# Four engines in a written order around attention and the Fourier mixer of a two-layer diffusion kernel

## The chip, the cores and the metric

The kernel is one program on one core of a Trainium2 chip. The core has five engines that run side by side, each working through its own list of instructions: PE (TensorE, matrix products; its weight loads are shown apart as PEld), DVE (VectorE), ACT (ScalarE), POOL (GpSimd) and SP (SyncE), which here only issues transfers. The metric is the device time of one execution in microseconds, from the first to the last moment of the program on the chip.

## What is computed

Two layers over 256 tokens of width 1024, in float32. Each layer is a mixer and a mixture of experts, both scaled, shifted and gated by "ada" vectors that come from a conditioning vector:

```python
for layer in range(2):
    mod = silu(c) @ ada_w[layer] + ada_b[layer]          # 6 vectors of 1024
    shift1, scale1, gate1, shift2, scale2, gate2 = split(mod, 6)
    h = modulate(rmsnorm(x, norm_mix[layer]), shift1, scale1)
    if layer == 0:
        q, k, v, xb, gb = split(h @ w_in)                # plus context keys and values
        attn = neighbourhood_attention(q, k, v, k_c, v_c, rpb)
        y = bidirectional_rglru(xc_lat, xc_ctx, ...)     # a scan in each direction
        mix = concat([attn, gelu(gb) * y]) @ w_out
    else:
        f = fft2(h in 4 channel groups, ortho).real      # over tokens and channels
        mix = f @ fnet_w_out
    x = x + gate1 * mix
    h2 = modulate(rmsnorm(x, norm_ffn[layer]), shift2, scale2)
    x = x + gate2 * grouped_moe(h2, ...)                 # best of 4 groups, its top 2 of 4 experts
```

## The kernel before, in words

Weights stream from memory through 16 slots of 1 MB in one fixed list that SP works off in order; a transfer starts when the slot that it needs has been released by its reader. A chunk of ada weights takes two slots and gives four columns of an ada vector (`modc`). A chunk is turned into numbers in one of three ways: on PE by 64 small products `gv` into one row, a copy to ACT's `gvr` and a second product that turns the row (`side(1)` takes one such chunk per attention unit, from the list `ADA`); on PE in the router by `fill` (the lists `FILL0`, `FILL1`); or on DVE in the slot itself with a column sum on PE (the list `BESIDE`).

The stages stand one behind the other. First the projections and the scan. Then attention in 20 units u: scores `s` in pairs, on DVE a bias add and a maximum `mx`, on ACT the exponential `P`, on DVE its division, on PE the transposes `pt`, copied by ACT to `PT`, and every fourth unit the product `av` of four units, which ACT and DVE (or POOL) split into a high and a low part `catH`, `catL`. From unit 6 on, one step of the output projection `mix` per unit stands between them: six products of 512 columns with a weight piece `wp` whose high part ACT copies and whose low part POOL or DVE subtracts, by the letters g and v of a string (`EO` in attention, `EF` in the Fourier mixer). Then the residual add (`gm`, `xt`), the norm, the router's logits `lg`, scores `sc`, the choice of experts `oh`, ranks `rk`, a selection matrix `S`, and the first gather `xg`, whose rows go to the first products `g`. Then eight pairs of experts (`g`, `u`, `dn`, scatter `ya`). Layer 1 begins with the Fourier mixer: `dr` (the transform matrix times the norm), `f`, `Y`, then `pq`, `pc`, `pn`, from which ACT and DVE make `fH` and `fL`, then sixteen `mix` steps; then the same router and experts.

What sets the order: PE's instructions stand as the program writes them from the projections to the end of the output projection (`by_hand`, line 699). All else, and the other engines throughout, is placed by a scheduler in the order in which it estimates that things become ready. The small row `dg`, made by POOL from an ada vector, is what PE turns into the gate row `gb` that ACT copies to `gate` for the residual add.

Of the kernel before, what the change touches and what calls it, by code (L numbers as in the profile page):

```python
# [36 lines left out]
ORDER = 'aaKaaBaGaaVaaapoa'  # L37
# [6 lines left out]
EF = 'vvggggvggvvggvgg'  # L44
# [101 lines left out]
def hybrid_layers(  # L146
# [73 lines left out]
    def exp_items(l):  # L220
# [137 lines left out]
    def ada_pe(l, j, ps_=gps, after=None):  # L358
        W = st.get(("a", l, j))
        return ada_te(l, [(W, q * 128, 4 * j + q) for q in range(4)], ps_=ps_, after=after, used=W.used)  # L360

# [10 lines left out]
    def ada_inplace(l, j):  # L372
# [4 lines left out]
        for k in range(1, 8):  # L377
            ve.scalar_tensor_tensor(r, W[:, k], sc32[:, k, 0:1], r, op0=ALU.mult, op1=ALU.add)
        W.done(1)
        yield  # L380
        p = wps("gv")
        for q in range(4):
            te.matmul(out=p[:, q:q + 1], lhsT=r[:, q * 128:(q + 1) * 128], rhs=ones[:, 0:1], start=True, stop=True)
        c4 = slice(4 * j, 4 * j + 4)
        ve.tensor_tensor(modc[l][:, c4], p[:, 0:4], ada_b[l][:, c4], op=ALU.add)
        W.done(0)
        yield
# [176 lines left out]
    st.add([ada_item(*a) for n in FILL0 for a in n])  # L564
# [134 lines left out]
    by_hand.enter_context(tc.manual_schedule(engines={mybir.EngineType.PE}))  # L699
# [51 lines left out]
    scan[1](99)  # L751
# [90 lines left out]
    def project(srcH, srcL, W, order, on):  # L842

        p = [acc("mix") for _ in range(4)]
        steps = [(k, h) for k in order for h in range(2)]
# [9 lines left out]
        for i, (k, h) in enumerate(steps):  # L855
            if i + 2 < 16:
                w[i + 2] = piece(i + 2)
            if i < 14:
                for tb in range(2):
                    c = slice(tb * 128, (tb + 1) * 128)  # L860
                    mm3(p[tb * 2 + h], (srcH[:, k, c], srcL[:, k, c]), w[i], i < 2, False)
            elif i == 15:
                for tb in range(2):
                    c = slice(tb * 128, (tb + 1) * 128)
                    for h in range(2):
                        mm3(p[tb * 2 + h], (srcH[:, k, c], srcL[:, k, c]), w[14 + h], False, True)
# [4 lines left out]
    mix = project(catH, catL, lambda h: st.get(("wo", h)), (4, 5, 6, 7, 0, 1, 2, 3), EO)  # L871
# [10 lines left out]
    gate = gate_rows(0, 16)  # L882
    for mp in mix:
        pass
    by_hand.close()


    def warm(n):

        p = gps("warm")  # L890
        for _ in range(n):
            te.matmul(out=p[:, 0:352], lhsT=ones, rhs=cst, start=True, stop=True)

    def add_mix(p4, gate):

        table(AF.Sqrt, p4[0][:, 0:1])
        ss = tn([128, 2, 2], "ssq")
        for h in range(2):
            c = slice(h * 512, (h + 1) * 512)
            for tb in range(2):  # L900
                add_gated(p4[tb * 2 + h], gate, tb, c)
                jk = t2k("jk")[:, 0:256].bitcast(BF16)
                ac.activation(jk, xt[:, tb, c], AF.Square, accum_out=ss[:, tb, h:h + 1])
        r = tn([128, 2], "rr", bufs=2)
        ve.tensor_tensor(r, ss[:, :, 0], ss[:, :, 1], op=ALU.add)
        ac.activation(r, r, AF.Sqrt, scale=1.0 / D, bias=eps)
        last = ve.reciprocal(r, r)
        return r, last

    def moe(l, r, store):  # L910
        a2 = scale_col(f"a2_{l}", modc[l], 32, g_ffn[l])
        b2 = modc[l][:, 24:32]

# [4 lines left out]
                         b2[:, :, None].to_broadcast([128, 8, 16]), op=ALU.mult)  # L918
# [4 lines left out]
        pre = table(AF.Sigmoid, r[:, 0:1])  # L923
        fins = fill(l, 0, pre)
        if not fins:
            warm(5)

        xT = t8k("xT").rearrange("p (k t) -> p k t", k=8)
        lg = acc("lg")
        lv = lg[:, 0:32].rearrange("p (t e) -> p t e", t=2)  # L930
        for kk in range(4):
            p = wps("tp")
            for i in range(4):
                k = 2 * kk + i // 2
                te.transpose(p[:, i * 128:(i + 1) * 128], xt[:, i % 2, k * 128:(k + 1) * 128], ident)
            pv = p.rearrange("p (k t) -> p k t", k=2)
            if kk % 2:
                ve.tensor_copy(xT[:, 2 * kk:2 * kk + 2], pv)
            else:
                ac.activation(xT[:, 2 * kk:2 * kk + 2], pv, AF.Copy)  # L940
        for k in range(8):
            for tb in range(2):
                at = te.matmul(out=lv[:, tb], lhsT=xT[:, k, tb * 128:(tb + 1) * 128], rhs=w2[:, k],
                               start=(k == 0 and tb == 0), stop=(k == 7 and tb == 1))
        for f in fins:
            f()
        with tc.issue_after(at.ins):
            fins = fill(l, 1, pre)
# [3 lines left out]
        for tb in range(2):  # L952
            ac.activation(xh[:, tb], xt[:, tb], AF.Copy, scale=r[:, tb:tb + 1])
            ve.scalar_tensor_tensor(xl[:, tb], xt[:, tb], r[:, tb:tb + 1], xh[:, tb].bitcast(F32),
                                    op0=ALU.mult, op1=ALU.subtract)
        sc = tn([128, 2, NE], "sc")
        for tb in range(2):
            ve.scalar_tensor_tensor(sc[:, tb], lv[:, tb], r[:, tb:tb + 1], crow, op0=ALU.mult, op1=ALU.add)
        ac.activation(sc, sc, AF.Sigmoid)
        table(AF.Silu, sc[:, 0, 0:1])  # L960
# [31 lines left out]
        warm(3)  # L992
# [6 lines left out]
        rank = tn([128, 2, NE], "rank")  # L999
        ve.scalar_tensor_tensor(rank, rk[:, 0:32].rearrange("p (t e) -> p t e", t=2), 1.0, oh, op0=ALU.add, op1=ALU.mult)  # L1000
# [5 lines left out]
        at = ve.scalar_tensor_tensor(over, rank, float(CAP), gates, op0=ALU.is_gt, op1=ALU.mult)  # L1006

        with tc.issue_after(at.ins):
            for f in fins:
                f()  # L1010
        sg_of = {}

        def gather(b):


            e = 4 * b
            S = t2k("S")[:, 0:512].bitcast(F32R)
# [360 lines left out]
```

## Time and profile before

| what | us |
|---|---|
| three runs, median (lowest, highest) | 807.3 (803.17, 809.81) |
| the profiled execution, its own time | 808.83 |
| its span, first to last instruction | 807.0 |
| attention and output projection, from the first scores | 172.9 to 247.35 |
| router of layer 0 and first gather | 247.35 to 274.27 |
| experts of layer 0 | 274.27 to 511.2 |
| Fourier mixer | 511.2 to 558.93 |
| router of layer 1 and first gather | 558.93 to 585.5 |
| experts of layer 1 and the store | 585.5 to 807.0 |

Times in the table after the third row are positions in the span, read from the trace. The profiled execution lies 1.5 us over the median, so a sum made against it is lowered by 1.5 us to compare it with the median.

### The profile page before, as it was taken

To read this page: it belongs to the slowest core of one execution; us is meant where nothing else is said; L and a number is where in the kernel's file an instruction comes from. 1 tells how busy PE (TensorE), PEld (TensorE's weight loads), DVE (VectorE), ACT (ScalarE), POOL (GpSimd) and SP (SyncE) were. 2 spreads that over 40 slices of the span, in tenths; PEclk is the share of its full clock that TensorE was granted. 3 is DMA by queue.
4 is the path that set the end of the run, shared out by engine and by line. 5 is a ranking of instruction groups with operands and counts; after the bars stand their busy time and mean duration, and the time that the engine had idled before them with its cause. 6 is when DMAs were issued, how large, how long until landed. Compare 5 with 4: busy or idle time off the path is not lost. (4 is left out here: it accounts for less than half of the span.)

```text
span 807.0 us, 11360 instructions
## 1 busy us (share of the span) xinstructions
PE 726.8 (90%) x4602; PEld 398.8 (49%) x4602; DVE 291.8 (36%) x577; ACT 243.8 (30%) x435; POOL 124.4 (15%) x107
## 2 busy tenths in 40 slices
PE   3999987976999899799999879699899799999996
PEld 2677576554777534244334324467643343444334
DVE  4558279185634321021143231444421110221115
ACT  6253975944556111010011000354310100110001
POOL 1146254353240001000000000023000000000002
PEclk8899999997999999899999989899899999999999
DMA  8999843495468799999999999974579999999995
GB/s 280 361 356 403 337 167 130 183 358 212 163 257 344 292 424 421 378 422 421 422 421 421 421 421 421 420 305 156 210 305 422 418 386 423 421 421 421 422 402 181
DMA packets 53793, 277.40 MB, mean 344 GB/s; under 512 B 4898, under 2 KB 20832, under 8 KB 22496
## 3 DMA queue, kind: packets, MB, share of 16 engines
q1 hardware_dynamic: 53008, 275.95, 85.4%
q8 instruction: 40, 0.66, 0.3%
q10 hardware_dynamic: 720, 0.59, 0.2%
q14 instruction: 25, 0.20, 0.1%
HBM read 275.47 MB, written 1.05 MB: 343 GB/s over the span
## 5 line engine op out<-in xcount | busy, mean ns | idle before, releaser
L1085 PE MATMUL g<-slot,xg 128*64 128x512 f32 x512 | 122.2, 627 | 13.3 <-PEq L1193 8.2
L1085 PE MATMUL u<-slot,xg 128*64 128x512 f32 x512 | 115.2, 593 | 3.9 <-DMA slot<-in_moe_u_dram 3.9
L1122 PE MATMUL dn<-slot,aT 128*64 128x512 f32 (+1 forms) x544 | 115.4, 571 | 3.2 <-DVE aT L1106 3.2
L392 POOL TENSOR_TENSOR wp<-slot,wp 128x512 fp32r<-128x512 f32 x52 | 73.5, 1420 | 157.0 <-ACT wp L391 156.9
L1085 PEld LDWEIGHTS g<-slot,xg 128*64 128x64 f32 x512 | 39.3, 145 | 91.9 <-issue 83.8
L1091 DVE TENSOR_TENSOR act<-act,u 128x512 f32<-128x512 f32 x16 | 11.0, 687 | 199.2 <-PE u L1085 199.2
L1085 PEld LDWEIGHTS u<-slot,xg 128*64 128x64 f32 x512 | 37.6, 137 | 78.1 <-issue 69.8
L1122 PEld LDWEIGHTS dn<-slot,aT 128*64 128x64 f32 x544 | 37.6, 137 | 69.0 <-issue 60.8
L1124 ACT ACTIVATE yH<-dn,gcol 128x512 fp32r<-128x512 f32 (+1 forms) x34 | 22.5, 662 | 139.1 <-PE dn L1122 133.7
L1042 POOL TENSOR_TENSOR SG<-S,gates 128x512 f32<-128x512 f32 x8 | 8.4, 1045 | 355.0 <-PE st L1094 307.3
L1040 ACT ACTIVATE xg<-xg,modc,a 128x256 f32<-128x256 f32 x32 | 18.0, 564 | 135.8 <-PE xg L1031 135.8
L1125 DVE SCALAR_TENSOR_TENSOR yL<-dn,gcol,yH 128x512 fp32r<-128x512 f32 (+1 forms) x34 | 24.4, 719 | 89.7 <-ACT yH L1124 81.5
L334 PE MATMUL gv<-slot,sc 128*32 128x128 f32 x1344 | 51.3, 292 | 4.0 <-ACT sc L307 2.0
L391 ACT ACTIVATE wp<-slot 128x512 fp32r<-128x512 f32 x72 | 44.5, 626 | 30.3 <-PE mix L406 9.3
L1090 ACT ACTIVATE act<-g 128x512 f32<-128x512 f32 x16 | 9.6, 597 | 132.9 <-PE g L1085 132.9
L334 PEld LDWEIGHTS gv<-slot,sc 128*32 128x32 f32 x1344 | 42.1, 118 | 14.5 <-issue 7.0
L1031 PE MATMUL xg<-S,xh 128*128 128x256 f32 x128 | 27.3, 295 | 3.3 <-DVE S L1019 2.1
L1038 DVE TENSOR_SCALAR xg<-xg,a,modc 128x256 f32<-128x256 f32 x32 | 17.4, 543 | 31.8 <-ACT xg L1040 31.8
L1062 PE MATMUL ya<-yH,ST 128*128 128x512 f32 x60 | 26.4, 440 | 0.3 <-ACT yH L1124 0.2
L1031 PE MATMUL xg<-S,xl 128*128 128x256 f32 x128 | 25.9, 284 | 0.0
L1062 PE MATMUL ya<-yL,ST 128*128 128x512 f32 x60 | 24.1, 402 | 0.6 <-DVE yL L1125 0.6
L392 DVE TENSOR_TENSOR wp<-slot,wp 128x512 fp32r<-128x512 f32 x20 | 16.9, 846 | 20.7 <-ACT wp L391 20.5
(269 smaller groups left out, 1101.0 us busy)
## 6 DMA issues: line engine op xcount, KB each, us to landing
slot<-in_moe_g_dram SPq DMA_DIRECT2D x64, 1024.0 KB, 14.2
slot<-in_moe_u_dram SPq DMA_DIRECT2D x64, 1024.0 KB, 15.1
slot<-in_moe_d_dram SPq DMA_DIRECT2D x60, 1024.0 KB, 16.2
slot<-in_ada_w_dram SPq DMA_DIRECT2D x40, 1024.0 KB, 8.3
slot<-in_w_in_dram SPq DMA_DIRECT2D x8, 1024.0 KB, 12.4
slot<-in_ada_w_dram SPq DMA_DIRECT2D x12, 512.0 KB, 9.1
slot<-in_w_out_dram SPq DMA_DIRECT2D x4, 1024.0 KB, 7.2
slot<-in_fnet_w_dram SPq DMA_DIRECT2D x4, 1024.0 KB, 19.8
```

The costliest lines, as they stand in the source:

```text
L334: te.matmul(out=p[32 * q:32 * q + 32, 0:128], lhsT=sc32[:, k, :], rhs=W[:, k, c:c + 128], start=(k == 0), stop=(k == 7))
L391: ac.activation(dst_h, src, AF.Copy)
L392: eng.tensor_tensor(dst_l, src, dst_h.bitcast(F32), op=ALU.subtract)
L1031: at_xg[0] = te.matmul(out=p[:, i * 256:(i + 1) * 256], lhsT=xx[:, tb, k * 128:(k + 1) * 128], rhs=S[:, tb * 256:(tb + 1) * 256], start=(n ...
L1038: ve.tensor_scalar(xg[:, k], pv, a2[:, k:k + 1], b2[:, k:k + 1], op0=ALU.mult, op1=ALU.add)
L1040: ac.activation(xg[:, k], pv, AF.Identity, scale=a2[:, k:k + 1], bias=b2[:, k:k + 1])
L1062: te.matmul(out=yacc[tb * 2 + h], lhsT=ST[:, tb * 128:(tb + 1) * 128], rhs=y[:, h * 512:(h + 1) * 512], start=(p == 0 and n == 0), stop=(n ...
L1085: te.matmul(out=q[half(i), :], lhsT=xg[:, k, half(i0 + i)], rhs=W[i][:, k], start=(k == 0), stop=(k == 7))
L1091: ve.tensor_tensor(act, act, gu[1], op=ALU.mult)
L1122: te.matmul(out=dn[half(i), :], lhsT=aT[:, fc * 128 + 64 * i:fc * 128 + 64 * i + 64], rhs=W[i][:, fc, c], start=(fc == 0), stop=(fc == 3))
L1124: ac.activation(yH[:, c], dn, AF.Copy, scale=gcol)
L1125: ve.scalar_tensor_tensor(yL[:, c], dn, gcol, yH[:, c].bitcast(F32), op0=ALU.mult, op1=ALU.subtract)
```

## The change

All four computing engines now keep the order in which the program writes their instructions, in two stretches: from the first attention unit to the first gather of layer 0, and from the Fourier mixer's start to the first gather of layer 1. The last nine steps of the second scan direction are called from units 0 to 2, three each. The output projection starts one step later against the units (13 steps beside units and not 14); residual adds are taken apart by half of the width (`add_part`), and in the Fourier mixer the steps are ordered so that the first half is done four steps before the end. The router's weights are made ready ahead of the norm, its products are taken in halves, and its filling products (`warm`) are fewer. Of the ada chunks two move into the list that attention takes (13 and not 11), three and not four are taken in the router of layer 0, and the last two are loaded behind the Fourier weights and reduced by DVE beside the mixer, where three were loaded among the experts of layer 0 and reduced there.

```diff
-ADA = [(0, 4), (0, 5), (0, 6), (0, 7), (0, 8), (0, 9), (1, 0), (1, 2), (1, 1), (1, 3), (1, 6)]
-FILL0 = [[(0, 10), (0, 11)], [(1, 4), (1, 5)], []]
-FILL1 = [[], [(1, 10), (1, 11)], []]
-BESIDE = [(1, j) for j in (7, 8, 9)]
-EF = 'vvggggvggvvggvgg'
+ADA = [(0, 4), (0, 5), (0, 6), (0, 7), (0, 8), (0, 9), (1, 0), (1, 2), (1, 1), (1, 3), (1, 6), (1, 7), (1, 4)]
+FILL0 = [(0, 10), (0, 11), (1, 5)]
+FILL1 = [(1, 10), (1, 11)]
+BESIDE = [(1, 8), (1, 9)]
+EF = 'gggvggvggvggvggv'
...
-            if l == 0 and n == "d" and p - 4 in range(len(BESIDE)):
-                r.append(ada_item(*BESIDE[p - 4]))
...
     st.add([st.chunk(("fw", h), fnet_w[h]) for h in range(2)])
-    st.add([ada_item(*a) for n in FILL1 for a in n])
+    st.add([ada_item(*a) for a in BESIDE + FILL1])
...
-    by_hand.enter_context(tc.manual_schedule(engines={mybir.EngineType.PE}))
+    by_hand.enter_context(tc.manual_schedule(engines={te.engine}))
+    engines = {te.engine, ve.engine, ac.engine, gp.engine}
...
-    scan[1](99)
+
+    by_hand.close()
+    by_hand.enter_context(tc.manual_schedule(engines=engines))
...
     for u in range(20):
         att()
-        if u < 6:
+        if u < 10:
             side(1)
-        if 2 <= u < 6:
+        scan[1](3 if u < 3 else 0)
+        if 3 <= u < 7:
             cat()
         if u >= 6:
-            mp = next(mix)
+            next(mix)
...
+        def low(h, tb):
+            c = slice(h * 512, (h + 1) * 512)
+            ve.scalar_tensor_tensor(xl[:, tb, c], xt[:, tb, c], r[:, tb:tb + 1], xh[:, tb, c].bitcast(F32),
+                                    op0=ALU.mult, op1=ALU.subtract)
...
-    warm(8)
-    r, _ = add_mix(yacc, gate)
+    by_hand.enter_context(tc.manual_schedule(engines=engines))
...
+    for tb in range(2):
+        add_part(yp, gate, 0, tb)
+    add_part(yp, gate, 1, 0)
+    warm(6, xt[:, 1, 0:352])
+    e0 = first_half()
+    rms(r, e0, 0)
+    add_part(yp, gate, 1, 1)
+    warm(4, xt[:, 0, 512:864])
+    rms(r, e0, 1)
...
+    group(0)
+    group(1)
+    next(mix)
     gate = gate_rows(1, 16)
-    for mp in project(fH, fL, lambda h: st.get(("fw", h)), range(8), EF):
-        pass
-    r, _ = add_mix(mp, gate)
-    moe(1, r, True)
+    lg = Logits()
+    for n, mp in enumerate(mix):
+        beside(1)
+        if n in (10, 11):
+            ada_sum(*BESIDE[n - 10])
+        if n == 11:
+            table(AF.Sqrt, eps)
+            for tb in range(2):
+                add_part(mp, gate, 0, tb)
+        if n == 12:
+            a2, crow = router_weights(1)
...
+    moe(1, mp, gate, lg, a2, crow, True)
```

ACT in the second half of attention, before (line 788 is the exponential of one unit, 804 the copy `PT`, 391 a high part):

```order
L788 ACTIVATE P,sm<-s,mx 128x512 x2
L391 ACTIVATE wp<-slot_1567 128x512
L804 ACTIVATE PT<-pt 128x4x128
L391 ACTIVATE wp<-slot_1567 128x512
L804 ACTIVATE PT<-pt 128x4x128
L788 ACTIVATE P,sm<-s,mx 128x512 x2
```

The same place of the kernel after (808, 824 and 408 are those lines there):

```order
L808 ACTIVATE P,sm<-s,mx 128x512
L824 ACTIVATE PT<-pt 128x4x128
L408 ACTIVATE catH<-av 128x256
L408 ACTIVATE wp<-slot_1628 128x512
L808 ACTIVATE P,sm<-s,mx 128x512
L824 ACTIVATE PT<-pt 128x4x128
L408 ACTIVATE wp<-slot_1628 128x512
```

Two exponentials stood side by side ahead of the pieces; now a copy `PT` and a piece `wp` stand between the two exponentials of every pair.

POOL at the start of the Fourier mixer's `mix`, before (420 is the gate's `dg`, 392 a low part; `SG` belongs to the experts ahead of it):

```order
L1042 TENSOR_TENSOR SG<-S,gates 128x512 x2
L420 TENSOR_TENSOR dg<-cst,modc_141 128x1024
L392 TENSOR_TENSOR wp<-slot_6878,wp 128x512 x2
L392 TENSOR_TENSOR wp<-slot_6880,wp 128x512 x3
```

POOL at the same place, after (437 and 409 are those lines):

```order
L1081 TENSOR_TENSOR SG<-S,gates 128x512 x2
L409 TENSOR_TENSOR wp<-slot_6874,wp 128x512 x2
L437 TENSOR_TENSOR dg<-cst,modc_141 128x1024
L409 TENSOR_TENSOR wp<-slot_6876,wp 128x512
```

ACT there, after:

```order
L1387 ACTIVATE fm<-pn 1x2x127
L408 ACTIVATE fH<-fm 128x2x256 x2
L408 ACTIVATE wp<-slot_6874 128x512 x2
L443 ACTIVATE gate<-gb 128x512 x2
L408 ACTIVATE wp<-slot_6876 128x512 x2
```

And PE there, after (1374 to 1376 are the last transform products, 421 to 423 the first `mix` step):

```order
L1374 MATMUL pq<-Y,dft 128x254
L1375 MATMUL pc<-Y,dft 128x258
L1376 MATMUL pn<-Y,dft 32x258
L442 MATMUL gb<-dg,cst 128x512 x2
L421 MATMUL mix<-wp,fH 128x512
L422 MATMUL mix<-wp,fH 128x512
L423 MATMUL mix<-wp,fL 128x512
```

The gate's `dg` stood on POOL ahead of the low parts, with nothing of the mixer before it; now it stands behind the first two low parts, whose high parts stand on ACT behind the last `fH`, and on PE the gate's products stand ahead of the first `mix` step.

## Rows read from the trace of the kernel before

**Rows 1.** Windows: us; busy PE, PEld, DVE, ACT, POOL; PEclk; DMA share; GB/s.

```profile
193.00:247.35 54.35, 52.63 (x408) 37.20 (x407) 26.69 (x64) 31.10 (x67) 16.05 (x12) 1.00 0.63 241
247.35:274.27 26.92, 24.31 (x354) 20.11 (x353) 15.10 (x45) 12.21 (x25) 1.05 (x1) 0.87 0.93 371
274.27:511.20 236.93, 220.18 (x1021) 90.76 (x1020) 56.99 (x97) 26.65 (x43) 6.92 (x5) 0.97 0.99 409
511.20:528.20 17.00, 9.52 (x34) 7.99 (x34) 9.47 (x25) 6.61 (x18) 1.27 (x1) 0.80 1.01 421
528.20:535.50 7.30, 7.30 (x29) 3.87 (x28) 3.15 (x9) 3.74 (x11) 0.00 (x0) 1.00 1.02 423
535.50:558.93 23.43, 23.01 (x98) 18.05 (x97) 8.46 (x13) 10.75 (x22) 11.71 (x9) 1.00 0.54 185
558.93:585.50 26.57, 22.94 (x233) 18.32 (x232) 13.78 (x41) 11.55 (x23) 1.05 (x1) 0.87 0.43 172
585.50:807.00 221.50, 207.36 (x1021) 86.43 (x1020) 46.49 (x87) 24.82 (x41) 10.00 (x8) 0.98 0.95 385
```

**Rows 2.** PE's timeline at attention's start: start, us, engine, line, operation.

```profile
173.96 1.95 PE L334 MATMUL gv<-slot,sc 128*32 128x128 f32 x64
187.01 0.47 PE L342 MATMUL gv<-cst,gvr 128*128 128x128 f32 x1 [11.10 <-ACT gvr L340]
187.41 2.39 PE L776 MATMUL s<-kq 64*128 64x256 f32 x8
189.74 3.15 PE L334 MATMUL gv<-slot,sc 128*32 128x128 f32 x64
```

**Rows 3.** PE's timeline in the steady units of attention.

```profile
207.64 1.14 PE L776 MATMUL s<-kq 64*128 64x256 f32 x8
208.70 0.66 PE L803 MATMUL pt<-cst,P 128*128 128x128 f32 x4
```

**Rows 4.** Groups by line on ACT, 193 to 247.35: busy, mean ns, idle before.

```profile
L391 ACT ACTIVATE wp<-slot 128x512 fp32r<-128x512 f32 x16 | 9.9, 627 | 3.8 <-PE mix L406 2.2 <-PE av L811 1.5
L804 ACT ACTIVATE PT<-pt 128x512 f32<-128x512 f32 x16 | 9.5, 596 | 14.0 <-PE pt L803 10.9 <-PE av L811 3.0
L788 ACT ACTIVATE P<-s,mx 128x512 f32<-128x512 f32 x12 | 8.1, 683 | 1.1 <-DVE mx L785 0.9
```

**Rows 5.** Groups by line on DVE, same stretch.

```profile
L785 DVE TENSOR_REDUCE mx<-s 128x1 f32<-128x512 f32 x12 | 7.7, 680 | 0.0
...
L783 DVE TENSOR_TENSOR s<-s,bg 128x256 f32<-128x256 f32 x12 | 4.8, 428 | 3.6 <-PE s L776 3.6
```

**Rows 6.** Groups by line on POOL, same stretch.

```profile
L392 POOL TENSOR_TENSOR wp<-slot,wp 128x512 fp32r<-128x512 f32 x11 | 14.2, 1295 | 38.5 <-ACT wp L391 38.5
L420 POOL TENSOR_TENSOR dg<-cst,modc 128x1024 f32<-128x1024 f32 x1 | 1.9, 1897 | 1.9 <-PE av L811 1.9
```

**Rows 7.** PE's timeline: the last product of layer 1's experts.

```profile
801.75 0.28 PE L1072 MATMUL z<-yL,ST 128*128 128x256 f32 x1
```

**Rows 8.** PE's timeline in the Fourier mixer.

```profile
518.70 9.49 PE L1260 MATMUL f<-dr,xt 128*128 128x257 f32 x32 [7.48 <-DVE dr L1251]
```

**Rows 9.** DVE's timeline in the Fourier mixer.

```profile
526.49 0.35 DVE L1262 TENSOR_SCALAR Y<-f,a 128x129 f32<-128x129 f32 x1 [0.32 <-PE f L1260]
527.35 0.35 DVE L1262 TENSOR_SCALAR Y<-f,a 128x129 f32<-128x129 f32 x1 [0.32 <-PE f L1260]
...
535.64 0.68 DVE L392 TENSOR_TENSOR fL<-fm,fH 128x512 fp32r<-128x512 f32 x1
537.32 1.36 DVE L392 TENSOR_TENSOR fL<-fm,fH 128x512 fp32r<-128x512 f32 x1 [1.00 <-ACT fH L391]
```

**Rows 10.** POOL's timeline in the Fourier mixer.

```profile
536.85 1.29 POOL L392 TENSOR_TENSOR wp<-slot,wp 128x512 fp32r<-128x512 f32 x1 [23.33 <-ACT wp L391]
```

**Rows 11.** PE's timeline in the router of layer 1.

```profile
564.53 4.79 PE L892 MATMUL warm<-cst 128*128 128x352 f32 x10
```

**Rows 12.** DVE's timeline in the router of layer 1.

```profile
571.19 2.47 DVE L954 SCALAR_TENSOR_TENSOR xl<-xt,rr,xh 128x1024 fp32r<-128x1024 f32 x2
```

More of the change, by code (lines that the diff above doesn't have):

```diff
@@ L386, in ada_inplace, with ada_parts @@
         W.done(0)
+    def ada_parts(l, j, p, stops=()):
+        W = st.get(("a", l, j))
+        for k in range(8):
+            for q in range(4):
+                te.matmul(out=p[32 * q:32 * q + 32, 0:128], lhsT=sc32[:, k, :], rhs=W[:, k, q * 128:(q + 1) * 128],
+                          start=(k == 0), stop=(k == 7))
+            W.used(k)
+            if k in stops:
+                yield
+        yield
+        r = t1k("gvr")
+        ac.activation(r[:, 0:128], p[:, 0:128], AF.Copy)
+        yield
+        te.transpose(p[:, 128:256], r[:, 0:128], ident)
+        yield
+        c4 = slice(4 * j, 4 * j + 4)
+        ve.tensor_tensor(modc[l][:, c4], p[:, 128:256:32], ada_b[l][:, c4], op=ALU.add)
         yield
@@ L840, in add_gated, with project @@
         eng.tensor_tensor(xt[:, tb, c], xt[:, tb, c], m[:, 0:n], op=ALU.add)
-    def project(srcH, srcL, W, order, on):
-        p = [acc("mix") for _ in range(4)]
-        steps = [(k, h) for k in order for h in range(2)]
+    def project(srcH, srcL, W, steps, on, last):
         def piece(i):
@@ new lines, in moe @@
+    def moe(l, p4, gate, lg, a2, crow, store):
+        b2 = modc[l][:, 24:32]
+        fills = (FILL0, FILL1)[l]
+        third = ada_parts(*fills[2], gps("gv"), (2, 5)) if len(fills) > 2 else iter(())
+        r = tn([128, 2], "rr", bufs=2)
+        add_part(p4, gate, 1, 0)
+        e0 = first_half()
+        rms(r, e0, 0)
+        if l == 0:
+            lg.turn(0, 0)
+            lg.turn(0, 1)
+            lg.copy(0, ac)
+            lg.copy(1, ac)
+        next(third, 0)
+        lg.products(0)
+        lg.turn(1, 0)
+        next(third, 0)
+        add_part(p4, gate, 1, 1)
+        rms(r, e0, 1)
+        lg.turn(1, 1)
+        lg.copy(2, ve)
+        lg.copy(3, ac)
+        ve.reciprocal(r, r)
+        table(AF.Sigmoid, eps)
+        next(third, 0)
+        lg.products(1)
+        pieces = [ada_parts(*a, wps("gv")) for a in fills[:2]]
+        for f in pieces:
+            next(f)
+        sc = tn([128, 2, NE], "sc")
+        for tb in range(2):
+            ve.scalar_tensor_tensor(sc[:, tb], lg.lv[:, tb], r[:, tb:tb + 1], crow, op0=ALU.mult, op1=ALU.add)
+        ac.activation(sc, sc, AF.Sigmoid)
@@ L991, in moe, with rows_of @@
         te.matmul(out=rk[:, 32:48], lhsT=cnt[:, 1], rhs=oh[:, 1], start=False, stop=True)
-        warm(3)
+        for f in (third, *pieces, third):
+            next(f, 0)
+        warm(2)
+        low(0, 0)
+        rank = tn([128, 2, NE], "rank")
+        ve.scalar_tensor_tensor(rank, rk[:, 0:32].rearrange("p (t e) -> p t e", t=2), 1.0, oh, op0=ALU.add, op1=ALU.mult)
+        def rows_of(e, n):
+            S = t2k("S")[:, 0:512].bitcast(F32R)
+            s4 = S.rearrange("p (t e c) -> p t e c", t=2, e=n)
+            ve.tensor_tensor(s4, iota1[:, None, None, :].to_broadcast([128, 2, n, 64]),
+                             rank[:, :, e:e + n, None].to_broadcast([128, 2, n, 64]), op=ALU.is_equal)
+            return S
@@ L993, in moe @@
+        for f in (third, *pieces):
+            next(f, 0)
         gates = tn([128, 2, NE], "gates")
@@ L1144, in moe @@
                 u = up(p, xg)
-                if l == 0 and p - 5 in range(len(BESIDE)):
-                    next(beside)
-                if p == 0:
-                    for f in fins:
-                        f()
                 if pend:
```

254 lines of the change are left out of this document (135 added, 119 removed).

## The prediction

> **What bounds the kernel now.** I read the windows by stage first [rows 1]. From 193 on attention is PE's: it is busy 52.6 of 54.4 us at a clock of 1.00 (2.4 GHz), while ACT has 31.1, DVE 26.7 and POOL 16.1 of work that hides beside it. The order that the scheduler gave the three other engines there costs almost nothing, so a written order can gain almost nothing in that stretch and can lose. The two routers (26.9 and 26.6 us) are chains through all engines; PE's busy share in them is partly filler, as in layer 1, where 4.79 us are `warm` products ahead of the logits [rows 11]. The experts of layer 0 take 236.9 us with the transfers at 0.99 of their full rate; the same eight pairs in layer 1 take 216.5 from 585.5 to their last product at 802.0 [rows 1, 7]. The difference is three ada chunks in layer 0's stream, six parts of 1.05 MB at 421 GB/s [rows 1], 2.5 us each, their column sums, and what is queued behind them. The Fourier mixer is 17.0 + 7.3 + 23.4 us: the end of the adds, the norm and `f`; the small transforms; sixteen `mix` steps of 1.46.
>
> **The change part by part**
>
> *Two more ada chunks in attention.* A chunk is 64 small products and one more, 1.95 and about 0.35 at full clock [rows 2]. PE has no gap for them: +4.6.
>
> *Scan's end spread, softmax order at the start.* PE stood 11.1 us for `gvr`, and the products after that wait ran at half clock: a score pair 2.39 and not 1.14, a chunk 3.15 and not 1.95 [rows 2, 3]. The chain of scan, maximum and exponential of the first units stays, and only its parts change places. Between -1.3 and +0.5; taken 0.
>
> *Written order on ACT in attention.* Before, both exponentials of a pair run side by side; now the copy `PT` and the piece `wp` stand between them. A `wp` waits for PE to end the `mix` step whose buffer it takes, and behind it waits the second exponential; without this, PE cannot reuse the bank of that score for the next `pt`. I followed four units from the end of an `av`. Behind it ACT copies `catH` (estimate 0.4) and a piece (0.63), DVE splits (0.4), adds (0.43) and takes the maximum (0.68), ACT exponentiates (0.68 and a read of 0.2) [rows 4, 5]; with 0.2 per hand-over the score is free 3.2 after the `av`, when PE has done one `mix` step and one score pair, 2.55: 0.65 idle. In the next pair the piece is released by the `mix` step at 6.85; piece 0.63, its low part on DVE 0.7, add, maximum, exponential end at 10.65, where PE was through at 8.0: 2.65 idle. With the low part on POOL (two of three pieces) it is about 1.5. With small waits between these the four units cost some 2.7 more. Three such cycles: 8. In units 3 to 6 the copy `gvr` of a chunk, which waits for PE, stands ahead of the exponential: 3.5. Together +11.5. From below it is 0, if PE stays the bound (ACT needs 4 x 2.1 of the 11.8 us that four units take now); from above +14, 2.65 in each pair of units. I take 11.5, since each wait was followed in the listed order with durations of [rows 3 to 5].
>
> *Router of layer 0.* One chunk less (-2.0), no `warm` ahead of the logits; but the low parts of the second half wait on DVE behind two modulations, and the copies for the logits on ACT behind a square. Followed instruction by instruction it takes 25.5 and not 26.9: -1.4, between -6 (these waits hidden) and +1 (half clock in the small products).
>
> *Experts of layer 0.* Without the six parts and their sums the stage is that of layer 1: 216 and not 236.9, -21. From below the transfers alone, -15; from above -23. PE and the stream are then about level, so nothing else is late by much.
>
> *Fourier, up to the last `f`.* The adds, the squares and the norm end about 0.7 earlier against the last scatter, although a table load (1.3, estimate from the loads of the routers) now stands between two squares. The ten `warm` products sit where PE stood 7.48, so `f` starts at full clock: its eight pieces come 0.86 apart as the later ones do, 7.0 and not 9.49 [rows 8, 9]. Together -3.1, between -0.7 and -4.
>
> *From the last `f` to the first `mix` step.* Before: 7.3 [rows 1], with the gate's `dg` made earlier. Now `dg` stands on POOL behind two low parts, these wait for high parts on ACT, and those stand behind the last `fH`. The last `fH` ends about 8.0 after `f`, the two high parts 9.1; POOL takes 1.3 + 1.3 + 1.9 [rows 6], to 13.2; the gate's two products on PE 1.3; the first step starts at 14.6. +7.3. PE has nothing to do from about 6.1 to 13.2. Nothing hides this, since `mix` stands behind the gate's products on PE. From below +3 (the small steps of ACT and DVE faster than I strung them), from above +9. Here the trace also shows a DVE operation with two inputs taking 1.36 and not 0.69 while POOL ran a low part from 536.85 to 538.14 [rows 9, 10]. The Trainium skill, "SBUF — State Buffer", section "Who interferes with whom", says that such a DVE operation and one of GpSimd lock each other out for the whole instruction. By it one reduction of an ada chunk on DVE could hold a low part back here, 0.7 more; the sum leaves it out.
>
> *The `mix` steps.* Sixteen at 1.46 as before, and between them: 8 small products of the two chunks (0.2 to 3.8 by [rows 2], taken 1.0), eight transposes and the product `cp` (1.9, estimate from `pt`'s 0.41 for four and one more), a wait of 2.1 for `cp`, whose input stands on DVE behind four adds of 0.65 that start at the end of step 11. After PE's gap of 7 us I expect half clock for a start, as after the gap of 11.1: 2.39 - 1.14 + 3.15 - 1.95 = 2.45 [rows 2, 3]. Together +7.0 (with 0.4 of `gb` that left), between +3 and +9. DVE's eight-fold sums (16 operations of about 0.65) and POOL's pieces (11 of 1.3 in 30 us) lie beside PE; if they did not, each late piece would cost up to 1.3.
>
> *Router of layer 1.* Half of the adds and of the logits lie beside `mix` now. The 4.79 of `warm` and the 2.47 of `xl` no longer stand ahead of the logits and of the second score [rows 11, 12]; the score is done about 9 earlier against the last step. But the two ada chunks on PE (3.9) end where the ranks start, and behind the selection the low parts stand on DVE behind two modulations, some 2.3 more. 20.5 and not 26.6: -6, between -9 and -3.
>
> *Experts of layer 1.* All 16 slots are full at its start before and after, so the shift carries to the end: 0, up to +3 if the stream is late.
>
> Sum: 4.6 + 11.5 - 1.4 - 21 - 3.1 + 7.3 + 7.0 - 6 = -1.1. From 808.8 that is 807.7, and 1.5 lower against the median of 807.3: **806**.
>
> **The rivals**
>
> *PE stays the bound in attention.* If the copies and pieces on ACT run so far ahead that the waits fall to about 2, attention costs 6.6 and not 16.1: 806 - 9.5 = 796. For it: ACT is busy 31 of 54 us. Against it: the order is written, and a piece cannot pass the `mix` step that frees its buffer.
>
> *The holes cost the clock.* PE's idle pieces of 0.6 to 2.7 us in attention let the clock fall to 1.2 GHz now and then, and what runs meanwhile doubles. The trace before shows half clock only after long gaps [rows 2]; from 193 on, with hardly a gap, it shows 1.00 [rows 1]. If a fifth of the 60 us of product time in attention ran at half clock, +12: 818. It decides from about 9 us of products at half clock, where the sum passes 815. The Trainium skill, "TensorE: Matmul & The Clock Gate", section "A second HAM failure mode: psum-queue depth-cycling", tells of a kernel whose products pause so often between groups that the clock falls and rises all through; by that rule it would come out so, and the trace before neither shows nor excludes it.
>
> *The Fourier hole is not there.* If `dg` ran ahead of the pieces after all, and full clock held, 7.3 and 2.5 go, and with waits in attention of half my figure 790. The order speaks against it.
>
> **How the numbers follow.** About 1% (8 us) is what a measurement of this kernel can tell from no change. My case, 799 to 815 with its centre at 806: 0.50. PE the bound in attention, 791 to 799: 0.24, and the third rival, about 790: 0.08; both faster by over 1%, 0.32. The clock, over 815: 0.18. The range that leaves out 0.2 is 790 to 818: the terms' bounds add up wider (-28 to +25 about the sum), but they are not at one end together.
>
> **What would show it.** In the trace after: attention's first scores to the last `mix` step 16 longer, with PE idle before `pt` and ACT's exponentials and pieces named as what ended it; no idle of PE over 3 in the experts of layer 0 but the branch's, and 216 for them; `f` in 7; PE idle for some 7 before `gb` in the Fourier mixer with POOL's `dg` named; `mix` there some 30; the second router 20 to 21. The prediction is wrong if attention's waits come out under 5 or over 16, if products there run at half clock, or if the experts of layer 0 still wait for transfers.

## The result and the profile after

The changed kernel takes 829.99 us in the median of four runs (827.03 to 834.2), the kernel before 806.22 beside it (four runs, one more than in the opening): a ratio of 1.0297, 95% interval 1.0248 to 1.0346. I had forecast 806 with a range to 818, so it is slower where I expected no change. The profiled execution has a span of 826.7, 19.7 over before.

The first view is the windows by stage of the kernel after, in the columns of [rows 1]: attention in two parts, router of layer 0, its experts, Fourier to the last `f`, the stretch to the first `mix` step, the `mix` steps, the second router, the experts of layer 1 with the store.

```profile
174.10:219.50 45.40, 30.27 (x335) 21.22 (x334) 23.18 (x46) 14.77 (x34) 11.22 (x12) 0.66 0.62 232
219.50:272.90 53.40, 44.43 (x352) 31.67 (x352) 23.11 (x55) 25.05 (x52) 13.40 (x10) 1.00 0.60 219
272.90:296.80 23.90, 18.19 (x284) 15.05 (x283) 12.77 (x36) 15.03 (x30) 0.00 (x0) 1.00 0.74 293
296.80:514.10 217.30, 207.47 (x980) 86.29 (x980) 39.97 (x73) 25.05 (x41) 6.07 (x5) 0.98 0.98 407
514.10:530.40 16.30, 15.10 (x54) 10.87 (x54) 8.89 (x26) 6.14 (x15) 0.00 (x0) 0.90 1.02 424
530.40:548.80 18.40, 9.11 (x29) 4.23 (x28) 9.44 (x20) 7.21 (x19) 4.85 (x3) 0.84 0.80 332
548.80:579.70 30.90, 27.14 (x126) 21.00 (x125) 23.48 (x27) 11.62 (x22) 13.64 (x9) 0.99 0.61 241
579.70:601.80 22.10, 17.91 (x213) 15.70 (x211) 11.37 (x33) 10.61 (x20) 0.00 (x0) 0.82 0.61 235
601.80:826.70 224.90, 210.83 (x1020) 88.68 (x1020) 47.37 (x92) 24.28 (x40) 11.07 (x9) 0.96 0.93 379
```

Two things stand out. Attention lasts 98.8 us and not 74.5, and its first half runs at a granted clock of 0.66. And the experts of layer 0 have indeed fallen to 217.3, so the change earns 19.6 there and loses more elsewhere.

The waits of PE in attention of the kernel after (who waited for whom, us in total, times, longest) answer to [rows 2 to 4], where a gap of 11.1 for `gvr` was nearly all:

```profile
PE pt L823 <- ACT P L808: 13.1, 8, 2.8
PE gv L332 <- ACT P L808: 4.4, 1, 4.4
PE gv L332 <- ACT PT L824: 2.1, 3, 0.7
PE s L796 <- ACT P L808: 1.3, 1, 1.3
```

The exponential `P` ends 18.8 of these waits. One of them, on ACT's timeline after, with DVE's behind it: the piece `wp` of line 408 stands between the two exponentials of a pair; its low part stands on DVE ahead of the second unit's add and maximum, and DVE waits 3.23 for it; PE's `pt` at 247.47 waits 2.14 for the exponential.

```profile
242.90 0.67 ACT L808 ACTIVATE P<-s,mx 128x512 f32<-128x512 f32 x1
...
244.18 0.63 ACT L408 ACTIVATE wp<-slot 128x512 fp32r<-128x512 f32 x1
246.63 0.69 ACT L808 ACTIVATE P<-s,mx 128x512 f32<-128x512 f32 x1 [1.83 <-DVE mx L805]
```

```profile
244.84 0.69 DVE L409 TENSOR_TENSOR wp<-slot,wp 128x512 fp32r<-128x512 f32 x1 [3.23 <-ACT wp L408]
245.45 0.42 DVE L803 TENSOR_TENSOR s<-s,bg 128x256 f32<-128x256 f32 x1
245.91 0.69 DVE L805 TENSOR_REDUCE mx<-s 128x1 f32<-128x512 f32 x1
```

PE's timeline in the early units after, to be read beside [rows 2]: each wait is shorter than the 11.1 before, but they go on, and the products between them take the time of half clock (3.64 for a chunk's 64, 2.22 for a score pair) as late as 196.

```profile
185.83 3.64 PE L332 MATMUL gv<-slot,sc 128*32 128x128 f32 x64 [4.38 <-ACT P L808]
192.27 1.12 PE L823 MATMUL pt<-cst,P 128*128 128x128 f32 x4 [2.80 <-ACT P L808]
193.18 0.42 PE L340 MATMUL gv<-cst,gvr 128*128 128x128 f32 x1
193.93 2.22 PE L796 MATMUL s<-kq 64*128 64x256 f32 x8 [0.32 <-DVE modc L351]
```

The Fourier mixer's start on PE after, which answers to [rows 8]: `f` takes 7.11 and not 9.49, but its start waits for nothing that the view names, because the fillers ahead of it run until 523.4 while its input was ready at 520.3. Then PE stands 8.45 for the gate's `dg`, and the gate's four passes take 3.75 and not the 1.88 of four at full clock.

```profile
515.26 8.17 PE L910 MATMUL warm<-xt,cst 128*128 128x352 f32 x20 [1.14 <-DVE xt L860]
...
523.27 7.11 PE L1357 MATMUL f<-dr,xt 128*128 128x257 f32 x32
...
545.99 3.75 PE L442 MATMUL gb<-dg,cst 128*128 128x512 f32 x4 [8.45 <-POOL dg L437]
```

POOL there, answering to [rows 6, 10]: the two low parts, then `dg`.

```profile
541.08 3.00 POOL L409 TENSOR_TENSOR wp<-slot,wp 128x512 fp32r<-128x512 f32 x2 [89.41 <-ACT wp L408]
544.04 1.89 POOL L437 TENSOR_TENSOR dg<-cst,modc 128x1024 f32<-128x1024 f32 x1
```

DVE in the same place: an operation of the ada chunk's reduction beside POOL's low parts, and the same operation later, with POOL idle.

```profile
541.21 1.75 DVE L372 SCALAR_TENSOR_TENSOR slot<-slot,sc,slot 128x512 f32<-128x512 f32 x1
...
568.77 0.74 DVE L372 SCALAR_TENSOR_TENSOR slot<-slot,sc,slot 128x512 f32<-128x512 f32 x1
```

### The profile page after: what moved, and what is told of

It is laid out like the page before. It is cut to its first block, busy times and chain, and to the rows that moved or that the text cites. A ratio compares the mean times of both kernels' runs of the same rounds, so it can differ in the third digit from the quotient of the medians.

```text
span 826.7 us, 11452 instructions
## 1 busy us (share of the span) xinstructions
PE 732.0 (89%) x4649; PEld 403.7 (49%) x4649; DVE 292.5 (35%) x571; ACT 249.2 (30%) x443; POOL 126.7 (15%) x108
## 5 line engine op out<-in xcount | busy, mean ns | idle before, releaser
L1173 PE MATMUL u<-slot,xg 128*64 128x512 f32 x512 | 112.8, 592 | 0.0
L409 POOL TENSOR_TENSOR wp<-slot,wp 128x512 fp32r<-128x512 f32 x53 | 77.0, 1460 | 223.9 <-ACT wp L408 223.7
L332 PE MATMUL gv<-slot,sc 128*32 128x128 f32 x1088 | 46.0, 309 | 9.7 <-ACT P L808 4.4
L332 PEld LDWEIGHTS gv<-slot,sc 128*32 128x32 f32 x1088 | 36.6, 124 | 20.3 <-issue 5.8
L409 DVE TENSOR_TENSOR wp<-slot,wp 128x512 fp32r<-128x512 f32 x19 | 21.6, 1137 | 21.4 <-ACT wp L408 21.3
L1150 PE MATMUL ya<-yL,ST 128*128 128x512 f32 x60 | 23.9, 398 | 1.4 <-DVE yL L1213 1.4
L823 PE MATMUL pt<-cst,P 128*128 128x128 f32 x64 | 11.6, 310 | 13.6 <-ACT P L808 13.1
L1133 PE MATMUL xg<-S,xh 128*128 128x256 f32 x96 | 19.8, 287 | 0.9 <-DVE S L1064 0.9
## 6 DMA issues: line engine op xcount, KB each, us to landing
slot<-in_w_in_dram SPq DMA_DIRECT2D x8, 1024.0 KB, 12.5
```

What stands on the lines that cost most here:

```text
L332: te.matmul(out=p[32 * q:32 * q + 32, 0:128], lhsT=sc32[:, k, :], rhs=W[:, k, c:c + 128], start=(k == 0), stop=(k == 7))
L409: eng.tensor_tensor(dst_l, src, dst_h.bitcast(F32), op=ALU.subtract)
L823: te.transpose(w[:, c * 128:(c + 1) * 128], P[:, c * 128:(c + 1) * 128], ident)
L1133: te.matmul(out=p[:, i * 256:(i + 1) * 256], lhsT=xx[:, tb, k * 128:(k + 1) * 128], rhs=S[:, tb * 256:(tb + 1) * 256], start=(n + tb == 0) ...
L1150: te.matmul(out=yacc[tb * 2 + h], lhsT=ST[:, tb * 128:(tb + 1) * 128], rhs=y[:, h * 512:(h + 1) * 512], start=(p == 0 and n == 0), stop=(n ...
L1173: te.matmul(out=q[half(i), :], lhsT=xg[:, k, half(i0 + i)], rhs=W[i][:, k], start=(k == 0), stop=(k == 7))
```

## The experiments

All runs compare with the kernel before, run beside them on the same chip. The table gives stage lengths in us from PE's timeline of each run's profile: first scores to last `mix` step (att), to the first expert product (r0), to the last scatter (moe0), to the first `f` (start), `f`, from it to the first `mix` step (hole), `mix`, second router (r1), experts of layer 1 to the last product (moe1). Each length is that of one execution. The stages up to attention's start and the first router differ by some us between executions with the same instructions there (first scores at 172.3 to 174.5; r0 at 23.9 to 30.3 in after, e2 and e4 to e9).

| run | att | r0 | moe0 | start | f | hole | mix | r1 | moe1 | median us | ratio to before (95%) |
|---|---|---|---|---|---|---|---|---|---|---|---|
| before | 74.5 | 26.8 | 236.9 | 7.5 | 9.5 | 7.3 | 23.6 | 26.4 | 216.5 | 806 to 809 | 1 |
| after | 98.8 | 23.9 | 217.3 | 9.1 | 7.1 | 18.4 | 30.9 | 22.1 | 219.7 | 829.99 | 1.0297 (1.0248 to 1.0346) |
| e1 | 79.9 | 20.4 | 215.5 | 7.4 | 7.1 | 18.4 | 31.2 | 22.1 | 220.0 | 802.92 | 0.9926 (0.9898 to 0.9953) |
| e2 | 100.1 | 28.8 | 217.1 | 7.8 | 7.1 | 8.9 | 29.6 | 18.3 | 215.3 | 813.74 | 1.0074 (1.0049 to 1.0099) |
| e3 | 79.2 | 20.4 | 217.7 | 7.8 | 7.1 | 8.8 | 29.6 | 18.3 | 215.3 | 787.53 | 0.9752 (0.9735 to 0.9770) |
| e4 | 100.0 | 30.3 | 220.3 | 7.5 | 7.1 | 12.8 | 33.1 | 22.1 | 216.7 | 828.99 | 1.0221 (1.0159 to 1.0282) |
| e5 | 91.1 | 27.7 | 217.3 | 9.0 | 7.1 | 18.4 | 30.8 | 22.1 | 219.2 | 822.12 | 1.0171 (1.0144 to 1.0197) |
| e6 | 98.4 | 26.4 | 217.7 | 7.5 | 7.1 | 18.4 | 33.0 | 22.0 | 218.7 | 828.11 | 1.0239 (1.0208 to 1.0270) |
| e7 | 93.9 | 27.8 | 217.5 | 9.1 | 7.1 | 18.4 | 30.9 | 22.1 | 219.2 | 827.11 | 1.0240 (1.0215 to 1.0265) |
| e8 | 92.2 | 27.7 | 217.4 | 9.2 | 7.1 | 18.4 | 30.9 | 22.1 | 219.6 | 826.16 | 1.0229 (1.0179 to 1.0280) |
| e9 | 90.5 | 27.8 | 217.6 | 7.5 | 7.1 | 12.8 | 31.8 | 20.5 | 216.6 | 816.01 | 1.0118 (1.0049 to 1.0188) |
| e10 | 98.9 | 28.6 | 216.0 | 6.2 | 7.1 | 18.4 | 30.7 | 22.0 | 215.4 | 824.46 | 1.0194 (1.0141 to 1.0247) |
| e11 | 79.5 | 22.2 | 215.7 | 9.1 | 7.1 | 8.9 | 27.4 | 21.6 | 215.5 | 787.75 | 0.9753 (0.9699 to 0.9806) |
| e12 | 80.5 | 23.7 | 215.5 | 6.7 | 7.7 | 9.0 | 29.6 | 19.4 | 215.1 | 787.23 | 0.9743 (0.9718 to 0.9767) |

The theories: (1) the written order of ACT, DVE and POOL makes PE wait, in attention and ahead of the Fourier `mix`; (2) those waits, and the fillers that the change cut, let PE's clock fall, which lengthens what runs after. The rivals: the moved work (two chunks more, the scan's end in the first units) does it, whatever the order; or single other causes, named with the runs.

**e1, e2 and e3: the order undone, in one stretch, in the other, in both.** The same line is changed ahead of attention (e1), ahead of the Fourier mixer (e2), and in both places (e3).

```diff
-    by_hand.enter_context(tc.manual_schedule(engines=engines))
+    by_hand.enter_context(tc.manual_schedule(engines={te.engine}))
```

> The changed kernel, but from attention's beginning to the first gather of layer 0 only PE keeps the written order, as before; everything else as changed. Theory 1 (the written order of ACT and DVE makes PE wait in attention, and these short waits also hold PE's clock at its lower level): the 98.7 us of attention and output projection fall to about 80 (74.5 as before and two more ada chunks, 4.6), full clock from about 195 on, the router of layer 0 one or two us longer; in all 812 to 818. Rival (the moved work does it: two more chunks and the scan's end among the first units, whatever the order): attention stays over 92 and the whole over 823.

> The changed kernel, but in the Fourier mixer and the second router only PE keeps the written order. Theory 1 (the order of POOL and ACT puts the gate's row behind the pieces): the 18.4 us between the last f and the first mix step fall to 7 to 10, the whole to 818 to 822. Rival (PE's own new order, gate product ahead of the first mix step and pn in one bank, keeps the hole): it stays over 14 and the whole over 826.

> The changed kernel with PE alone in written order in both stretches: what is left of the change is the moved ada chunks, the split adds and routers and the fewer filling products. Theory 1: about the sum of the two single undoings, 800 to 808, so at or under the kernel before, since the experts of layer 0 keep the 19.6 us that they won. Rival (moved work): over 820.

e1: attention falls to 79.9, as theory 1 had it, and the whole by 27 to 803, more than I expected, since the router of layer 0 falls too, to 20.4, where I had expected it longer. e2: the hole falls to 8.9, the second router to 18.3 and the experts behind it to 215.3; the whole to 813.7, under the 818 to 822 expected. The two add up: e3 is at 787.5, under the 800 to 808 expected, and 2.5% faster than before. So the moved work does not lose where only PE's order is written: what is left of attention over before in e1 is 5.4, about the 4.6 of two chunks. PE's waits in attention in e3, to be read beside those of after: none for an exponential.

```profile
PE gv L340 <- ACT gvr L338: 11.5, 2, 11.1
PE gv L332 <- ACT PT L824: 2.1, 3, 0.7
PE s L796 <- DVE modc L351: 0.2, 1, 0.2
```

The whole windows of attention split the 18.9 us that the order costs there, first of e1, then of after, both with the same products on PE:

```profile
172.50:252.40 79.90, 66.14 (x687) 48.21 (x687) 44.88 (x97) 37.35 (x84) 24.61 (x22) 0.91 0.73 283
```

```profile
174.10:272.90 98.80, 74.70 (x686) 52.89 (x686) 46.29 (x100) 39.83 (x86) 24.62 (x22) 0.84 0.61 225
```

PE is busy 8.6 longer in after with the same products, at a mean clock of 0.84 and not 0.91, and idle 24.1 and not 13.8: 8.6 of clock and 10.3 of waits.

**e4: the gate's row ahead of the small transforms.**

```diff
+    gate = gate_rows(1, 16)
     group(0)
     group(1)
     next(mix)
-    gate = gate_rows(1, 16)
```

> The changed kernel with one line moved: the gate's row and its products of the Fourier mixer are written ahead of the small transforms and not behind the first two pieces; all engines still keep the written order. Theory 1 (dg behind two low parts on POOL, then gb at the lower clock): the 18.4 us from the last f to the first mix step fall to 12 to 13, the whole to 823 to 825. Rival (the chain to fH and the pieces alone sets it): it falls by under 3, the whole stays over 827.

The hole falls to 12.8, as theory 1 had it. The whole hardly moves (829.0, 819.6 to 831.0) and lies over the 823 to 825 expected: in the profiled execution the first router took 30.3, the experts of layer 0 220.3, and `mix` 33.1, since its first products now ran at half clock, behind the wait that is left. The wait, and the granted clock of the whole `mix` (0.99 in after):

```profile
552.26 0.74 PE L421 MATMUL mix<-wp,fH 128*128 128x512 f32 x1 [3.79 <-ACT wp L408]
```

```profile
552.30:585.40 33.10, 30.33 (x125) 24.21 (x125) 25.59 (x29) 11.55 (x22) 17.33 (x11) 0.85 0.69 277
```

So `dg` and `gb` are 5.6 of the 11.1 that the hole grew; the rest is the chain to the last `fH` and its pieces, for which PE still waits here; e2, where ACT, DVE and POOL are placed by the scheduler, has 8.9 in all.

**e5 and e6: which wait blocks ACT.** e5 writes the exponentials side by side, e6 makes a piece one step ahead (attention's call passes 1 for `lead`).

```diff
+            if u % 2 and u < n:
+                softmax(u - 1)
+                softmax(u)
             if 0 <= u - 1 < n:
-                softmax(u - 1)
```

```diff
-    def project(srcH, srcL, W, steps, on, last):
+    def project(srcH, srcL, W, steps, on, last, lead=2):
...
-        w = {i: piece(i) for i in range(2)}
+        w = {i: piece(i) for i in range(lead)}
...
-            if i + 2 < 16:
-                w[i + 2] = piece(i + 2)
+            if i + lead < 16:
+                w[i + lead] = piece(i + lead)
```

> The changed kernel, all engines in written order, but in attention the add, maximum and exponential of a pair's second unit are written right behind those of the first, one unit earlier, so that the second exponential stands ahead of the copy and the weight piece. Theory 1 (the second exponential behind copy and piece is what PE waits for): the 13.1 us of waits of pt for the exponential fall to under 5, attention from 98.8 to 84 to 90, the whole to 814 to 821. Rival A (the piece that waits for PE's mix step blocks ACT wherever the exponential stands): attention stays over 94.

> The changed kernel, but in attention's output projection a weight piece is made one step ahead and not two, so that its buffer is long free and ACT does not wait for the mix step beside it. Rival A (that wait blocks ACT): attention falls by 5 or more from 98.8, the whole to 825 or less. Theory 1 (the place of the second exponential): attention within 3 of 98.8, or longer since PE may wait for a late low part.

e5 takes 7.7 out of attention, to 91.1, between the 84 to 90 expected and the rival's 94. In its steady units, 219.5 to 250, PE is busy 28.8 of 30.5 us (23.3 in after), so there the place of the second exponential was the cause:

```profile
219.50:250.00 30.50, 28.75 (x197) 20.00 (x185) 17.02 (x37) 17.05 (x38) 7.70 (x6) 1.00 0.60 239
```

In the early units a single wait of 7.0 has come in place of shorter ones, and `pt` still waits 12.4 in all, not under 5. e6 hardly changes attention (98.4): the piece's wait for PE's `mix` step, which the prediction named, is not what sets its length. The waits of `pt` for exponentials fall from 13.1 to 9.3 there, and other waits take their place, 1.8 of them for low parts.

**e7: fillers where PE waits in attention.**

```diff
             if u < n and u % 2 == 0:
                 scores((u, u + 1))
+            if 2 <= u < 10:
+                fillp = gps("warm")
+                for _ in range(2):
+                    te.matmul(out=fillp[:, 0:352], lhsT=ones, rhs=cst, start=True, stop=True)
```

> The changed kernel with two filling products per unit in units 2 to 9, written between the scores and the transposes, where PE waits; sixteen of 0.59 at full clock, 9.4 us of work that adds nothing to the result. Theory 2 (PE's short idle pieces hold the clock at 1.2 GHz to 219): the clock in 196 to 219 rises from 0.67 to over 0.9 and attention falls from 98.8 to 90 to 95 in spite of the added work. Rival B (the clock there has another cause): the clock stays under 0.75 and attention is 100 to 110.

The clock, first of after, then of e7, in the same two windows:

```profile
196.00:208.00 12.00, 8.82 (x94) 6.26 (x97) 5.11 (x16) 4.12 (x10) 3.03 (x4) 0.64 0.49 176
208.00:219.50 11.50, 9.03 (x91) 6.09 (x83) 0.96 (x3) 3.68 (x9) 3.18 (x3) 0.69 0.52 182
```

```profile
196.00:208.00 12.00, 10.25 (x160) 7.38 (x159) 4.27 (x14) 4.14 (x11) 3.04 (x4) 1.00 0.47 178
208.00:219.50 11.50, 9.61 (x87) 5.94 (x90) 4.36 (x11) 5.03 (x12) 3.18 (x3) 1.00 0.74 274
```

With 9.4 us of useless work added, attention is 4.9 shorter, and the clock is 1.00 from 191 on. Theory 2 holds for this stretch: with its pauses filled, PE ran at full clock. The whole falls by only 2.9, since the router of layer 0 took 27.8 in this execution and 23.9 in that of after.

**e8: the scan whole ahead of the first unit.**

```diff
     hq(99)
+    scan[1](99)
```

> The changed kernel with the second scan's last nine steps called together ahead of the first unit, as before. Theory 1 (order and clock, not the spreading): attention within 4 of 98.8 and the whole within 1% of the changed kernel's 830. Rival C (the scan's steps between the first softmaxes start the slow clock): attention falls under 92, the whole under 823.

Attention falls by 6.6 to 92.2: neither under 92, as rival C had it, nor within 4. The whole, 826.2, is within 1%, with a first router of 27.7. All of attention, and a part of it:

```profile
173.50:265.70 92.20, 68.62 (x687) 49.49 (x687) 43.43 (x99) 39.22 (x85) 23.67 (x22) 0.94 0.64 241
187.80:215.10 27.30, 17.05 (x261) 12.25 (x255) 11.09 (x31) 11.81 (x29) 7.83 (x9) 1.00 0.71 265
```

PE's idle time is that of after (23.6 and 24.1); its product time for the same work falls by 6.1, from 74.7. So under a written order the spread of the scan's end cost clock, not waiting, and rival C's mechanism is there. In after, DVE takes three scan steps between the maxima of two units, from 185.5 to 190.3, and the early waits of PE are 1.3, 4.4 and 2.8; here they are one of 5.7 and one of 1.1. Behind it the clock is back at 1.00 by 187.8 and stays there to 215.1, although PE idles 10.3 of these 27.3 us, in waits of up to 2.5. So pauses alone do not tell the clock: the same kind of pauses stood at half clock in after. The rest, 12, stays.

**e9: another written order.** The edits of e4, e5, e7 and e8 together.

> The changed kernel with all four engines still in a written order, but a better one: the scan whole ahead of the first unit, the exponentials of a pair side by side, two filling products per unit in units 2 to 9, and the gate's row ahead of the small transforms. Theories 1 and 2 together (it is this order and the clock that it lets fall, not the writing of an order): attention falls from 98.8 to 81 to 86, the step from f to mix from 18.4 to 12 to 13, the whole to 804 to 812. Rival (a fixed order loses by itself, since what becomes ready first varies): attention stays over 89, the whole over 815.

All four engines keep a written order, and the waits of `pt` for exponentials are down from 13.1 to 1.4; the hole is 12.8 and the whole 816.0. Attention is 90.5, not 81 to 86: the sixteen fillers are about 9.4 of it, now that PE waits little, and one wait of 6.8 behind the scan is left.

```profile
PE s L797 <- DVE modc L351: 6.8, 1, 6.8
PE pt L824 <- ACT P L809: 1.4, 2, 1.1
```

```profile
174.10:264.60 90.50, 77.97 (x719) 53.61 (x719) 46.36 (x99) 39.08 (x85) 23.25 (x22) 0.94 0.65 246
```

By its numbers the result is the rival's (attention over 89, the whole over 815). Its reason is not borne out in attention, where PE idles 12.5 us, and 13.8 in e1 with the scheduler's order. A better order wins back 14 of the 24; that one exists which matches the scheduler's is not shown, and e3 is 28.5 faster than this one.

**e10: fillers moved.** Five ahead of `f` and not ten, three in each first gather.

```diff
-    warm(6, xt[:, 1, 0:352])
+    warm(3, xt[:, 1, 0:352])
...
-    warm(4, xt[:, 0, 512:864])
+    warm(2, xt[:, 0, 512:864])
...
+                if n and kk == 2:
+                    warm(3)
```

> The changed kernel with filling products moved: five and not ten ahead of f, and three in each router's first gather, where PE waits 1.9 for the low parts. Theory 2 (the clock at the expert stages' start is what the cut fillers cost; and the ten ahead of f run into f's start): layer 1's experts fall from 219.7 to 216 to 217, layer 0's from 217.3 to 215 to 216, the start of f comes 1.5 to 2.5 earlier but f takes 0.5 to 2 longer; the whole 823 to 827. Rival (the expert stages are longer for another cause, the stream): they stay within 0.5.

The start of layer 1's experts, first after, then e10:

```profile
601.80:606.00 4.20, 4.20 (x10) 1.35 (x12) 2.34 (x8) 0.00 (x0) 1.04 (x1) 0.50 0.02 4
```

```profile
602.10:606.30 4.20, 3.92 (x20) 1.65 (x21) 2.62 (x11) 0.00 (x0) 1.04 (x1) 1.00 0.02 4
```

Twice the products in the same 4.2 us. Layer 1's experts fall by 4.3, layer 0's by 1.3, `f` starts 2.9 earlier and stays at 7.1; the whole falls by 5.5. For layer 1's experts theory 2 holds here as well: the stream is not the cause. But the cut fillers do not explain it alone: e2 and e3 cut them too and have 215.3, at full clock from the stage's start, with the scheduler's order. Layer 0's 1.3 is not told apart from the spread of that stage (217.7 in e3, which also starts it at full clock).

**e11 and e12: PE alone in written order, refined.** e11 adds to e3 the gathers' fillers, e4's edit and `pn` in its old bank pool; e12 adds e10's edits to e3.

> PE alone in written order in both stretches, as in the run that undid both, and with three small edits: fillers in the first gather, the gate's row ahead of the small transforms, pn in the bank pool that it had before. If the wait of 1.2 for pn's bank and the clock at the experts' start still cost there: 2 to 5 under that run's 787.5, so 782 to 786. If the scheduler hides them: within 1% of it.

> PE alone in written order in both stretches, with the fillers as in the run that moved them: five ahead of f, three in each first gather. If the fillers do there what they did under four written orders (1.3 of layer 0's experts, 2.9 of the start of f), 783 to 786 against 787.5; if the scheduler has hidden them already, within 0.5% of 787.5.

Neither is told apart from e3 (787.75 and 787.23 beside 787.53). What the fillers give at the experts' start, the scheduled order had mostly already. The best version found is e3 in all three forms, about 2.5% faster than before: the moved chunks, with PE alone in a written order.

## Why the prediction was wrong

The step that failed is the price of the clock. I put half clock into the sum at one place, 2.45 at the head of the Fourier `mix`, and made the rest of it a rival with a chance of 0.18. The reason I gave against it, that the trace before shows half clock only after long gaps, was a wrong reading: [rows 1] have the two routers at 0.87, and in the first of them the clock stood at 0.50 behind a stretch in which PE was busy 5.3 of 5.7 us, with small products, and no wait was over 0.42.

```profile
248.00:253.70 5.70, 5.26 (x81) 4.59 (x74) 4.98 (x9) 3.43 (x10) 0.00 (x0) 1.00 1.03 430
253.70:257.10 3.40, 3.40 (x60) 2.87 (x61) 1.12 (x4) 2.31 (x4) 0.00 (x0) 0.50 0.69 289
```

By stages, measured against [rows 1] and beside the forecast:

- *Attention*, +24.3 and not +16.1. The waits were sized right in total: 10.3 measured (e1 against after) for 11.5, and the chunks 5.4 for 4.6. Left out were the 8.6 that the products took longer; the clock was at half in 30.7 of the 37.6 us from 180.9 to 218.5, between waits of 0.3 to 4.4 us. Most of it came in by a term that I took at 0, within -1.3 and +0.5: the spread of the scan's end cost 6.6 (e8). The prediction's rival had the clock at 12. The rule that it cites from the Trainium skill ("TensorE: Matmul & The Clock Gate", "A second HAM failure mode: psum-queue depth-cycling") agrees with the first half of attention: with pauses between groups the granted clock fell and rose, 0.66 over 45 us, and with the pauses filled it was 1.00 from 191 on (e7). Behind 219, and in e8 from 188 to 215, pauses of up to 2.5 us went with 1.00. My account of the wait was half wrong: the second exponential's place binds in the steady units (e5), the piece's wait for the `mix` step does not (e6). The 0.2 per hand-over is shown by no row; in the timelines above ACT's exponential starts 0.03 behind DVE's maximum (246.60 and 246.63). The projections also ended 1.2 later, within the spread of the other runs.
- *Router of layer 0*, -2.9 for -1.4, with luck: the clock in after's profile was 1.00 there, and seven other profiles with the same instructions took 26.4 to 30.3. The scheduler's order is worth more than I gave it: 20.4 in e1 and e3.
- *Experts of layer 0*, -19.6 for -21: right. The stage moved 96.9 MB before and 88.4 after, at nearly the same rate (time by GB/s of the windows); no run undoes that move alone. This is the gain that e3 keeps.
- *Fourier to the last `f`*, -0.8 for -3.1. `f` took 7.1 as forecast, but it stood behind ten fillers, which ran their first part at half clock and ended 2.9 after `f`'s input was ready. At full clock the same ten ended 1.2 after it (e1, e4, e6, e9), so 1.7 is the clock's.
- *The hole*, +11.1 for +7.3. The mechanism was the forecast one and PE stood for `dg` 8.45; the chain to the pieces on ACT was 2.0 longer than I strung it, and the gate's products cost 2.8 and not 1.3, at half clock. The port lock that I left out shows as 3.00 for two low parts that take 2.6 alone [rows 6]: 0.4, for the 0.7 that I had estimated by the rule of the Trainium skill ("SBUF — State Buffer", "Who interferes with whom"). The trace agrees that the two engines hold each other up: DVE's operation took 1.75 beside POOL's and 0.74 alone.
- *The `mix` steps*, +7.4 for +7.0: the size was right by luck. The clock was 0.99, so the 2.45 was not there (it came in e4). In its place were 1.3 for a late low part and 2.2 for the chunks' small products that I had at 1.0; the 1.9 for transposes and `cp`, which does not follow from the 0.41 that it names, was 1.2.
- *Router of layer 1*, -4.3 for -6: the two chunks' products took 5.8 for 3.9, at a clock of 0.62.
- *Experts of layer 1*, +3.4 for 0. I had named a late stream as what could cost there; 2.9 of it was the clock, 0.50 from the start to 607.6, where the router's fillers were cut and the order was written (e10, e2).

The span came out 19.7 over before, where the sum had -1.1. Of these 20.8 the half clock that was not in the sum is 8.6 + 1.7 + 1.5 + 1.9 + 2.9 = 16.6, against 2.45 that was in it where there was hardly any; the longer chain ahead of the hole, the later start and the late low part are most of the rest. (The bounds of the terms add up to -32 and +24 about the sum, not to the -28 and +25 stated; nothing hangs on it.) That a written order costs more than it gives here was the right reading; that its waits cost only their own length was not.

## What to carry to other kernels

Moving work out of a stage bound by transfers paid here at once (19.6 us for about 5), and writing the order of the helper engines by hand took it back: check for each written order which instruction stands ahead of the one that the bound engine waits for. Price a wait of TensorE twice, once by its length and once by the products that follow it at half clock; and before half clock is ruled out, look up every stretch at half clock in the trace before, and what TensorE did ahead of it. Before filler products are cut, see which stage's start they kept at full clock; before they are added, see whether they end ahead of what stands behind them.

## What was not expected of the hardware

- With waits of 0.3 to 4.4 us between busy pieces the granted clock was at half in 30.7 of 37.6 us (after, from 180.9), while behind a single gap of 11.1 us, in e1 and before, it was back at 1.00 after some 5 us of work, at 192. The shorter waits in a row cost more than the long one. But e8 has as much idle time in attention, in similar waits, and full clock from 187.8 to 215.1; what decides between the two is not shown.
- The same instructions of the first router took 23.9 us in the profile of after and 27.7 in that of e5, at a mean clock of 1.00 and of 0.81.
